# A hybrid decoder layer on one core: weight sums of the first four feed forward gemms made during the in-projection, and embedding stores on ScalarE's queue

## The chip, the cores and the metric

The kernel runs on one core of a Trainium2 chip. The metric is the device time of one execution in microseconds (us). A core has five engines with a queue of their own each: TensorE (PE in the profile, with its weight loads as PEld), VectorE (DVE), ScalarE (ACT), GpSimd (POOL) and SyncE (SP, which here only issues DMAs). Every queue is worked off in order; engines wait for one another through semaphores.

## The reference, cut to what matters

One layer, D_MODEL = 1024, 1024 rows, float32, D_FF = 2816:

```python
h = rms_norm(x, norm1_g)
proj = h @ w_in                                  # columns for three causal mixers
mixed = concat(gated_deltanet(...), multiscale_pool(...), short_gated_conv(...))
x = x + mixed @ w_out
h = rms_norm(x, norm2_g)
ff = silu(h @ w_gate) * (h @ w_up)
x = x + ff @ w_down
x = x + sigmoid(x @ ple_gate) * (p @ ple_proj)   # p: per-layer input embedding, 256 wide
return rms_norm(x, final_g)
```

## The kernel before, in words

All matrices stand transposed, 128 features on the partitions and the 1024 rows in two halves of 512. A float32 product is made of three matmuls, hi·hi, hi·lo and lo·hi: each operand is split into `hi`, a copy that ScalarE rounds (`act.copy` into an fp32r tile), and `lo`, the rest, which VectorE subtracts (`vec.tensor_tensor`). A matmul takes 128 x 128 weights and 512 columns.

The stages follow each other: the in-projection, with DeltaNet, pooling and short convolution woven into it; the out-projection (16 gemms of 24 matmuls, blocks of `w_out` split one ahead into `wh` and `wl`); the second norm; the feed forward gemms; the down-projection; the embedding gate and the last norm.

The feed forward is done by a 2 x 2 block scheme with seven products in place of eight. Its right operands `B[0]` to `B[6]` (four pieces each) come from the normed input: `B[0]`, `B[1]` from the first half of the rows alone, `B[2]` to `B[6]` from both. `norm2(1)` (L1231) makes them on VectorE in this order, and its events `t2_ev` and `t4_ev` stand for the end of what `B[2]` and `B[6]` are made of. The left operands of one of 22 gemms (`jobs`, even: two blocks of `w_gate`, odd: two of `w_up`) are two raw quarters a11, a12, four sums of quarters, and a22, with the numbers i = 0 to 6. The sums are four GpSimd instructions over 128 x 512, in `sums(n)` (L1338). Each of the seven operands is then split by ScalarE and VectorE into one of 8 `op` tiles, in the order of the list `uses`, and one operand feeds 12 matmuls, so a gemm has 84 matmuls.

`EARLY = 4`: the first four gemms start with products 0 and 1 (`head1`, `head2`), which need only `B[0]`, `B[1]`, while `norm2(1)` runs. Then come `embed(0)` (the first half of p @ ple_proj, 48 matmuls, whose operands go through the same `op` tiles), then products 2 to 6 of gemms 0 and 1 alternately (`p6`, `p7`, `p5`, `tail1`, `tail2`; the last needs `B[6]`), then `embed(1)`, then gemms 2 to 21. The sums of gemms 2 and 3 wait for `t4_ev`, and the first four `op` tiles used are given back only after `t4_ev` (`held_ops`, L1408). `embed_evac` (L1445) copies a block of 128 x 512 out of PSUM on ScalarE and stores it to `pp_d` in DRAM by SyncE; it is read again at the embedding gate.

Raw weight blocks of 512 KB lie in `wr` tiles: two in the pool `stg` (`ra_slots`) and four in `ffp` (`rb_slots`). Gemms 0 and 1 hold two `rb` slots each until their last operand is split; every later gemm holds one of each. `down_sums(p)` (L1579) takes two `rb` slots too, loads two blocks of `w_down`, makes four sums on GpSimd and stores them to `wd_d`; `a_sums(p)` (L1562) makes four GpSimd sums of the feed forward's activations, which SyncE stores to `a_d`. `after(n)` (L1664) starts one or the other behind gemm n.

The program order on every queue is written out by a planner, `Flow`: Python generators yield the time at which they go on by the planner's cost model, and a gemm's `fl.tick` advances its clock. The planner fixes the order of instructions; at run time each queue only waits for its semaphores. A DMA that SyncE can't issue yet, since its tile is not free, holds up all that stand behind it. Units of 128 x 512 in SBUF come from one pool of 69 (`gen`).

Of the kernel before, what the change touches and what calls it, by code (L numbers as in the profile page):

```python
# [9 lines left out]
F32 = mybir.dt.float32  # L10
F32R = mybir.dt.float32r
AF = mybir.ActivationFunctionType
ALU = mybir.AluOpType
# [8 lines left out]
NH = 4  # L22
NT = 8
NFF = 22
EPS = 1e-6

V_N1, V_N2, V_FG, V_TAP, V_STAP, V_PS, V_ON = 0, 8, 16, 24, 72, 78, 80
# [168 lines left out]
def kernel(  # L196
# [28 lines left out]
    x1_d = scr.tile([2, KT, P, HALF], F32, name="x1_d")  # L225
    a_d = scr.tile([7, NFF // 2, P, HALF], F32, name="a_d")
    wd_d = scr.tile([4, NFF // 2, P, HALF], F32, name="wd_d")
    pp_d = scr.tile([2, KT, P, HALF], F32, name="pp_d")

    uid = [0]  # L230
# [5 lines left out]
    def unit(dtype=F32, shape=(P, HALF)):  # L236
        return gen.tile(list(shape), dtype, tag="u", name=nm("u"))

    def load(src):
        t = unit(shape=tuple(src.shape))  # L240
        sync.dma_start(out=t, in_=src)
        return t
# [11 lines left out]
    def free(ps):  # L254

        if id(ps) in held:
            held.remove(id(ps))
            fl.spawn(mm_slots.later(), fl.left() - 0.15)

    def store(dst, src, ev):  # L260

        sync.dma_start(out=dst, in_=src)
        ev.set(2.6)
        yield 0
# [46 lines left out]
    class Weights:  # L311
# [5 lines left out]
        def fetch(self):  # L317
            if self.srcs and len(self.raw) < 2:
                src, kind = self.srcs.pop(0)
                raw = stg.tile([P, KT, P], F32, tag="wr", name=nm("wr"))  # L320
                sync.dma_start(out=raw, in_=src)  # L321
                self.raw.append((raw, kind))
# [183 lines left out]
    def gates(ab_sb):  # L506
# [75 lines left out]
        for pr in range(2):  # L582
            batch = list(zip(todo, ws))[4 * pr:4 * pr + 4]
            for (h, hf), w in batch:
                for t in range(4):
                    vec.tensor_scalar(out=w[:, t, :], in0=w[:, t, :], scalar1=gc[:, hf * 4 + t, h:h + 1],
                                      scalar2=None, op0=ALU.subtract)
                act.activation(out=w, in_=w, func=AF.Abs)
                yield from fl.calm(pr, "act", "vec")
            for (h, hf), w in batch:  # L590
                act.activation(out=w, in_=w, func=AF.Exp, scale=-1.0)
                fl.spawn(store(q4(w_d[h, hf]), w, w_done[h]), fl.left())
            yield fl.left()


    def conv_evac(tap, dst, ready):
# [690 lines left out]
    NPR = NFF // 2  # L1287
    jobs = []
    for p in range(NPR):
        jobs += [(w_gate[2 * p], w_gate[2 * p + 1]), (w_up[2 * p], w_up[2 * p + 1])]  # L1290


    EARLY = 4
    uses = []
    for n in range(0, EARLY, 2):
        uses += [(n, 0), (n + 1, 0), (n, 1), (n + 1, 1)]

    uses += [(-1, q) for q in range(4)]
    uses += [(b, i) for i in range(2, 7) for b in range(2)]
    uses += [(-1, q) for q in range(4)]  # L1300
    for n in range(2, len(jobs)):
        more = EARLY <= n + 1 < len(jobs)
        uses += [(n, 2), (n, 3), (n, 4)] + [(n + 1, 0)] * more + [(n, 5)] + [(n + 1, 1)] * more + [(n, 6)]
# [11 lines left out]
    def raw_tile(hp):  # L1315
        return hp.tile([P, KT, P], F32, tag="wr", name=nm("wr"), bufs=2 if hp is stg else 4)

    def weights():
        raws = [[None, None, Event(fl), Event(fl)] for _ in jobs]

        def fetch(n, c):
            raws[n][c] = raw_tile(ffp if c or n < 2 else stg)
            sync.dma_start(out=raws[n][c], in_=jobs[n][c])
            raws[n][2 + c].set(5.0)

        def loader():
            todo = [(n, c) for n in range(2) for c in range(2)] + [(2, 0), (3, 0), (2, 1), (3, 1)]
            todo += [(n, c) for n in range(4, len(jobs)) for c in range(2)]
            for n, c in todo:
                if n >= 2 and c == 0:  # L1330
                    yield out_w
                    yield from ra_slots.take()
                else:
                    yield from rb_slots.take()
                fetch(n, c)
                yield 0.1

        def sums(n):  # L1338
            if 2 <= n < EARLY:
                yield t4_ev  # L1340
            yield raws[n][2]
            yield raws[n][3]
            ra, rb = raws[n][0:2]
            a11, a12, a21, a22 = ra[:, 0:4], ra[:, 4:8], rb[:, 0:4], rb[:, 4:8]
            s1 = unit(shape=(P, 4, P))
            pool.tensor_tensor(out=s1, in0=a21, in1=a22, op=ALU.add)
            pool.tensor_tensor(out=a21, in0=a11, in1=a21, op=ALU.subtract)
            own[n] = (a11, a12, a11, a21, s1, a12, a22)
            yield split_ev[n]
            pool.tensor_tensor(out=a11, in0=s1, in1=a11, op=ALU.subtract)  # L1350
            pool.tensor_tensor(out=a12, in0=a12, in1=a11, op=ALU.subtract)
            yield fl.left()
            sum_ev[n].set()

        own = [None] * len(jobs)
        split_ev, sum_ev = events(len(jobs)), events(len(jobs))
        fl.spawn(loader())
        started = 0
        todo = [q for n, q in uses if n < 0]

        def proj(q):
            t = unit(shape=(P, 4, P))
            sync.dma_start(out=t.rearrange("p (k j) c -> p k (j c)", k=2),
                           in_=ple_proj[:, :, 2 * P * q:2 * P * q + 2 * P].rearrange("k p c -> p k c"))
            return t, fl.now + 4.0

        ahead = [proj(todo.pop(0)) for _ in range(2)]
        for n, i in uses:
            while started < len(jobs) and started <= n + 1:
                fl.spawn(sums(started))  # L1370
                started += 1
            yield from op_slots.take()
            if n < 0:
                raw, at = ahead.pop(0)
                yield max(0.0, at - fl.now)
                if todo:
                    ahead.append(proj(todo.pop(0)))
            elif i < 2:
                yield raws[n][2]
                raw = raws[n][0][:, 4 * i:4 * i + 4]  # L1380
            else:
                if i == 2:
                    yield t2_ev
                yield sum_ev[n]
                raw = own[n][i]
            hi, lo = op_tile()
            act.copy(out=hi, in_=raw)
            vec.tensor_tensor(out=lo, in0=raw, in1=hi.bitcast(F32), op=ALU.subtract)
            ops.append((hi, lo))
            if n >= 0 and i == 1:  # L1390
                split_ev[n].set()
            if op_free:
                op_free.pop().set()
            raw = None
            if i == 6:
                own[n] = raws[n] = None
                (rb_slots if n < 2 else ra_slots).give()
                rb_slots.give()
            yield 0.3

    def next_op():
# [43 lines left out]
    def embed_evac(ps, hf, j):  # L1445
        t = unit()
        act.copy(out=t, in_=ps)
        free(ps)
        yield fl.left()
        yield from store(pp_d[hf, j], t, pp_ev[hf][j])  # L1450

    def embed(hf):
        fl.until(pH_ev[hf])
        for q in range(4):
            hi, lo = next_op()
            for b in range(2):
                ps = bank()
                products(ps, [(hi[:, 2 * k + b], lo[:, 2 * k + b]) + tuple(pH[hf][k]) for k in range(2)])
                fl.spawn(embed_evac(ps, hf, 2 * q + b), 0.3)
            op_used()  # L1460
        pH[hf] = None
# [117 lines left out]
    def down_sums(p):  # L1579

        yield from rb_slots.take()
        yield from rb_slots.take()
        da, db = (raw_tile(ffp).rearrange("p k c -> p (k c)") for _ in range(2))
        sync.dma_start(out=da, in_=w_down[2 * p])
        sync.dma_start(out=db, in_=w_down[2 * p + 1])
        s1 = unit()
        yield 4.0
        a11, a21, a12, a22 = da[:, 0:HALF], da[:, HALF:], db[:, 0:HALF], db[:, HALF:]
        pool.tensor_tensor(out=s1, in0=a21, in1=a22, op=ALU.add)
        pool.tensor_tensor(out=a21, in0=a11, in1=a21, op=ALU.subtract)  # L1590
        pool.tensor_tensor(out=a11, in0=s1, in1=a11, op=ALU.subtract)
        pool.tensor_tensor(out=a12, in0=a12, in1=a11, op=ALU.subtract)
        yield fl.lag("pool")
        for i, t in enumerate((a11, a21, s1, a12)):
            sync.dma_start(out=wd_d[i, p], in_=t)
        rb_slots.give()
        rb_slots.give()
# [66 lines left out]
    def after(n):  # L1664
        p, _, ab = todo[n]
        if ab:
            fl.spawn(a_sums(p, *ab), 0.4)
        else:
            fl.spawn(down_sums(p), 2.0)

    g = [t[1] for t in todo]
    for n in range(0, EARLY, 2):
# [2 lines left out]
            f(g[n + 1])  # L1675
    embed(0)
    fl.spawn(p_proc(1))
    for f in (Gemm.p6, Gemm.p7, Gemm.p5, Gemm.tail1, Gemm.tail2):
        f(g[0])
        f(g[1])  # L1680
    after(0)
    after(1)
    embed(1)
    for n in range(2, len(g)):
        nxt = g[n + 1] if EARLY <= n + 1 < len(g) else None
        if n + 1 == len(g):
# [220 lines left out]
```

## Time and profile before

| what | value |
|---|---|
| median of 3 runs | 1254.97 us (1253.57 to 1256.13) |
| profiled execution, its own time | 1256.83 us |
| its span | 1255.2 us |
| TensorE busy | 1217.2 us, 97% of the span |
| VectorE, ScalarE, GpSimd busy | 64%, 42%, 25% |

The profile is of one execution. Stretches are given in microseconds from the start of its span. In a row, `x90` is a count of instructions; `<-DVE u` names the engine and the tile that ended a wait; the clock is TensorE's granted clock as a share of its full speed; SPq is SyncE's queue, where a row gives the time of issue. Names of tiles have no numbers, so `u` is any of the 69 units.

### The profile page before, as it was taken

How to read it: one execution, taken by the hardware profiler on the slowest of the kernel's cores; microseconds unless marked ns; L12 is line 12 of the kernel's file. 1: busy time of each engine (PE TensorE's matmuls, PEld its weight loads, DVE VectorE, ACT ScalarE, POOL GpSimd, SP SyncE). 2: the span in 40 equal slices, each digit the busy share in tenths (PEclk: the TensorE clock that was granted, in tenths of full speed). 3: DMA queues.
4: the chain of work that ended last, by engine and by line, in shares of the span. 5: the costliest groups of instructions: out<-in, count | busy, mean ns of one | idle time of the engine just before them, and what ended most of it. 6: DMA issues, size and time to landing. Idle time of an engine off the chain costs nothing.

```text
span 1255.2 us, 17243 instructions
## 1 busy us (share of the span) xinstructions
PE 1217.2 (97%) x6103; PEld 1006.8 (80%) x6103; DVE 801.1 (64%) x1381; ACT 527.5 (42%) x1114; POOL 308.2 (25%) x257
## 2 busy tenths in 40 slices
PE   8999999999999989978999999999999999999996
PEld 6778888888877878857888888888888888888886
DVE  8675886985766587865555555555547565553674
ACT  7256343254244343632333333333346444443553
POOL 7100001100010030074655655556530000000001
PEclk9999999999999999988999999999999999999998
DMA  6046353332335752345453543444369666563452
GB/s 223 17 144 187 102 136 101 107 101 85 100 130 166 253 182 84 126 158 180 154 188 127 191 145 151 160 176 143 132 221 373 205 213 198 174 197 116 146 181 94
DMA packets 112806, 196.63 MB, mean 157 GB/s; under 512 B 23696, under 2 KB 38864, under 8 KB 112720
## 3 DMA queue, kind: packets, MB, share of 16 engines
q1 hardware_dynamic: 112720, 195.53, 47.0%
q8 instruction: 48, 0.79, 0.3%
q14 instruction: 38, 0.31, 0.1%
HBM read 141.19 MB, written 54.30 MB: 156 GB/s over the span
## 4 chain that ended last, share of the span: by engine, by line
PE 52%; DVE 1%; DMA 1%; issue 0%; ACT 0%; POOL 0%; SPq 0%; POOLq 0%; ACTq 0%
PE dn L347 36%; PE mm L347 16%; DMA wr<-in_ple_gate_dram 1%; DVE u L140 1%; ACT u L140 0%; POOL u L140 0%; POOLq L1902 0%; DVE dl L140 0%; SPq L1817 0%; SPq L1798 0%; DVE ms L140 0%; POOL rs L140 0%; POOLq L140 0%; SPq L321 0%; ACTq L140 0%
## 5 line engine op out<-in xcount | busy, mean ns | idle before, releaser
L347 PE MATMUL dn<-u,op 128*128 128x512 f32 x1632 | 382.3, 394 | 12.8 <-DVE u L140 10.5
L347 PEld LDWEIGHTS dn<-u,op 128*128 128x128 f32 x1632 | 310.5, 191 | 80.5 <-DVE u L140 12.1
L347 PE MATMUL mm<-u,wh 128*128 128x512 f32 x1104 | 354.3, 402 | 5.4 <-DVE u L140 3.6
L140 DVE TENSOR_TENSOR u<-u,u 128x512 fp32r<-128x512 f32 (+2 forms) x358 | 234.6, 694 | 47.1 <-ACT u L140 40.4
L347 PEld LDWEIGHTS mm<-u,wh 128*128 128x128 f32 x1104 | 202.7, 190 | 49.1 <-DVE u L140 5.4
L347 PE MATMUL mm<-u,wl 128*128 128x512 f32 x552 | 217.9, 395 | 4.1 <-DVE wl L140 4.1
L140 ACT CAST u<-u 128x512 fp32r<-128x512 f32 x214 | 125.3, 620 | 137.4 <-DVE u L140 60.3
L140 DVE TENSOR_TENSOR op<-wr,op 128x512 fp32r<-128x512 f32 x132 | 121.0, 921 | 95.4 <-ACT op L140 93.8
L347 PE MATMUL dn<-u,u 128*128 128x512 f32 (+2 forms) x850 | 159.5, 336 | 0.0
L347 PEld LDWEIGHTS dn<-u,u 128*128 128x128 f32 (+1 forms) x850 | 123.6, 170 | 24.1 <-issue 0.5
L347 PEld LDWEIGHTS mm<-u,wl 128*128 128x128 f32 x552 | 104.7, 190 | 27.9 <-DVE wl L140 5.8
L140 ACT CAST op<-wr 128x512 fp32r<-128x512 f32 x132 | 81.5, 620 | 93.4 <-PE dn L347 58.8
L140 ACT ACTIVATE u<-u 128x512 f32<-128x512 f32 (+1 forms) x137 | 82.0, 605 | 88.3 <-DVE u L140 86.4
L347 PE MATMUL mm<-u,u 128*128 128x512 f32 (+1 forms) x522 | 112.0, 352 | 2.0 <-DVE u L140 1.5
L140 DVE TENSOR_TENSOR u<-dn,u 128x512 f32<-128x512 f32 x93 | 64.0, 689 | 73.6 <-PE dn L347 64.8
L140 DVE TENSOR_TENSOR wl<-wr,wh 128x512 fp32r<-128x512 f32 (+2 forms) x96 | 68.0, 711 | 65.0 <-ACT wh L140 64.4
L140 ACT COPY u<-dn 128x512 f32<-128x512 f32 (+4 forms) x99 | 47.7, 482 | 139.1 <-PE dn L347 139.1
L140 POOL TENSOR_TENSOR rs<-ms,mhalf 128x4 f32<-128x4 f32 (+1 forms) x7 | 6.6, 942 | 396.2 <-DVE ms L140 396.2
L347 PEld LDWEIGHTS mm<-u,u 128*128 128x128 f32 x522 | 85.5, 189 | 16.3 <-DVE u L140 2.1
L140 POOL TENSOR_TENSOR u<-u,u 128x512 f32<-128x512 f32 (+1 forms) x61 | 84.1, 1392 | 33.0 <-DVE u L140 20.4
L140 DVE TENSOR_TENSOR u<-mm,u 128x512 f32<-128x512 f32 x60 | 41.2, 687 | 48.2 <-PE mm L347 45.2
L140 ACT CAST wh<-wr 128x512 fp32r<-128x512 f32 (+2 forms) x96 | 57.7, 608 | 29.0 <-issue 12.5
(164 smaller groups left out, 1178.7 us busy)
## 6 DMA issues: line engine op xcount, KB each, us to landing
a_d<-u SPq DMA_DIRECT2D x77, 256.0 KB, 2.8
u<-a_d SPq DMA_DIRECT2D x77, 256.0 KB, 3.7
wr<-in_w_gate_dram SPq DMA_DIRECT2D x22, 512.0 KB, 4.6
wr<-in_w_up_dram SPq DMA_DIRECT2D x22, 512.0 KB, 4.5
wr<-in_w_down_dram SPq DMA_DIRECT2D x22, 512.0 KB, 4.9
u<-wd_d SPq DMA_DIRECT2D x44, 256.0 KB, 3.0
wr<-in_w_in_dram SPq DMA_DIRECT2D x21, 512.0 KB, 3.6
wd_d<-wr SPq DMA_DIRECT2D x33, 256.0 KB, 2.4
```

The lines of the kernel that those rows point to most:

```text
L140: return f(*a, **kw)
L347: pe.matmul(out=out, lhsT=lhsT, rhs=rhs, start=start, stop=stop, **kw)
```

## The change: what it does

A generator `early_sums`, started when the first norm's second half is done, loads the blocks of gemms 0 to 3 in quarters, makes their four sums each on GpSimd and stores them to `sd_d` in DRAM. At the feed forward, the operands of these gemms come from DRAM: tiles with key "a" (a11, a12), "s" (two sums), "d" (a22) and "e" (two pieces of `ple_proj`, which had units before) are fetched into the four `rb` slots in the order of use, each given back after its second split. From gemm 4 on, an even gemm holds both `ra` slots and an odd one two `rb` slots. `embed(1)` stands ahead of the two `tail2` of gemms 0 and 1. Embedding stores are issued by ScalarE. `down_sums` of pairs 0 and 1 go behind gemms 4 and 8.

```diff
+    def early_sums():
+        yield rs_done[1]
+        for n in range(EARLY):
+            wa, wb = gate_up(n)
+            a11, a12, a21, a22 = (load(w[:, r]) for w in (wa, wb) for r in (slice(0, 4), slice(4, 8)))
+            s1 = unit(shape=(P, 4, P))
+            yield 4.0
+            pool.tensor_tensor(out=s1, in0=a21, in1=a22, op=ALU.add)
+            pool.tensor_tensor(out=a21, in0=a11, in1=a21, op=ALU.subtract)
+            pool.tensor_tensor(out=a11, in0=s1, in1=a11, op=ALU.subtract)
+            pool.tensor_tensor(out=a12, in0=a12, in1=a11, op=ALU.subtract)
+            yield fl.left() + 2.0
+            for i, t in enumerate((a11, a21, s1, a12)):
+                sync.dma_start(out=sd_d[n, i // 2, :, 4 * (i % 2):4 * (i % 2) + 4], in_=t)
+            sd_ev[n].set(3.0)
+
+    fl.spawn(early_sums())
...
     uses += [(-1, q) for q in range(4)]
-    uses += [(b, i) for i in range(2, 7) for b in range(2)]
-    uses += [(-1, q) for q in range(4)]
+    uses += [(b, i) for i in range(2, 6) for b in range(2)]
+    uses += [(-2, q) for q in range(4)]
+    uses += [(b, 6) for b in range(2)]
...
+        def fetch_early(key):
+            t = tiles[key][0] = raw_tile(ffp)
...
+            elif key[0] == "s":
+                sync.dma_start(out=t, in_=sd_d[key[1], key[2]])
+            elif key[0] == "d":
+                sync.dma_start(out=t[:, 0:4], in_=jobs[key[1]][1][:, 4:8])
+            else:
+                sync.dma_start(out=t, in_=jobs[key[1]][0])
+            tiles[key][1].set(4.5)
+
         def fetch(n, c):
-            raws[n][c] = raw_tile(ffp if c or n < 2 else stg)
+            raws[n][c] = raw_tile(ffp if n % 2 else stg)
...
+        def loader(odd):
+            for key in tiles if odd else ():
+                if key[0] == "s":
+                    yield sd_ev[key[1]]
+                yield from rb_slots.take()
+                fetch_early(key)
                 yield 0.1
+            yield out_w
+            for n in range(EARLY + odd, len(jobs), 2):
+                for c in range(2):
+                    yield from (rb_slots if odd else ra_slots).take()
+                    fetch(n, c)
+                    yield 0.1
 
         def sums(n):
-            if 2 <= n < EARLY:
-                yield t4_ev
...
     def embed_evac(ps, hf, j):
         t = unit()
         act.copy(out=t, in_=ps)
+        act.dma_start(out=pp_d[hf, j], in_=t)
         free(ps)
-        yield fl.left()
-        yield from store(pp_d[hf, j], t, pp_ev[hf][j])
+        pp_ev[hf][j].set(4.0)
+        yield 0
...
         if ab:
             fl.spawn(a_sums(p, *ab), 0.4)
-        else:
+        elif n >= EARLY:
             fl.spawn(down_sums(p), 2.0)
+            if n < 3 * EARLY and n % 4 == 0:
+                fl.spawn(down_sums(n // 4 - 1), 20.0)
...
-    for f in (Gemm.p6, Gemm.p7, Gemm.p5, Gemm.tail1, Gemm.tail2):
+    for f in (Gemm.p6, Gemm.p7, Gemm.p5, Gemm.tail1):
         f(g[0])
         f(g[1])
+    embed(1)
+    g[0].tail2()
+    g[1].tail2()
     after(0)
     after(1)
-    embed(1)
```

## Rows read from the trace of the kernel before

**Rows 1.** Chain that ended last, pieces of a later gemm: start, us.

```profile
597.13 16.32 PE dn L347 x72
613.45 2.72 PE mm L347 x12
```

**Rows 2.** Stretches: PE busy, PEld, DVE, ACT, POOL (counts), clock, DMA share, GB/s.

```profile
440.00:460.00 20.00, 16.10 (x64) 12.61 (x63) 17.74 (x20) 8.81 (x18) 9.70 (x7) 0.91 0.45 152
...
500.00:520.00 20.00, 20.00 (x90) 16.57 (x89) 17.23 (x29) 16.87 (x32) 0.00 (x0) 1.00 0.36 132
520.00:540.00 20.00, 16.14 (x65) 12.43 (x64) 19.44 (x27) 6.29 (x12) 7.68 (x5) 0.92 0.42 132
540.00:560.00 20.00, 20.00 (x82) 16.16 (x80) 13.18 (x10) 7.93 (x15) 16.53 (x12) 0.91 0.36 109
560.00:580.00 20.00, 11.73 (x35) 8.88 (x35) 6.98 (x9) 4.64 (x8) 8.27 (x6) 0.74 0.73 273
```

**Rows 3.** What PE waited for, 430 to 475: total, times, longest.

```profile
PE mm L347 <- DVE wl L140: 3.9, 2, 2.7
```

**Rows 4.** What PE waited for, 530 to 600.

```profile
PE dn L347 <- DVE u L140: 10.5, 3, 6.2
PE dn L347 <- ACT u L140: 1.6, 1, 1.6
```

**Rows 5.** Timeline of all engines, 441 to 452: start, us.

```profile
441.94 1.78 DVE L140 TENSOR_TENSOR u<-u,u 128x512 fp32r<-128x512 f32 x1
...
443.13 1.75 POOL L140 TENSOR_TENSOR wr<-u,wr 128x512 f32<-128x512 f32 x1
...
451.02 0.68 DVE L140 TENSOR_TENSOR wl<-wr,wh 128x512 fp32r<-128x512 f32 x1
...
451.75 0.80 PE L347 MATMUL mm<-u,wl 128*128 128x512 f32 x1 [2.66 <-DVE wl L140]
```

**Rows 6.** DVE by form, 485 to 530, no sums on POOL: total, mean ns.

```profile
L140 DVE TENSOR_TENSOR u<-u,u 128x512 fp32r<-128x512 f32 x18 | 12.2, 687 | 0.0
```

**Rows 7.** DVE by form, 530 to 560, beside sums on POOL.

```profile
L140 DVE TENSOR_TENSOR op<-wr,op 128x512 fp32r<-128x512 f32 x6 | 8.1, 1395 | 2.6 <-ACT op L140 2.6
```

**Rows 8.** Timeline of all engines, 530 to 575.

```profile
532.17 1.52 POOL L140 TENSOR_TENSOR u<-wr 128x512 f32<-128x512 f32 x1 [49.22 <-ACT op L140]
...
537.64 6.17 PE L347 MATMUL dn<-u,op 128*128 128x512 f32 x14 [2.20 <-DVE u L140]
...
543.65 11.08 PE L347 MATMUL mm<-ph,op 128*128 128x512 f32 x48
...
563.18 0.58 ACT L140 COPY u<-mm 128x512 f32<-128x512 f32 x1 [7.27 <-DMA pp_d<-u]
...
566.41 5.04 PE L347 MATMUL dn<-u,op 128*128 128x512 f32 x12 [6.23 <-DVE u L140]
...
573.48 20.93 PE L347 MATMUL dn<-u,op 128*128 128x512 f32 x84 [2.04 <-DVE u L140]
```

**Rows 9.** SP's issues in the same stretch: start, us.

```profile
545.85 0.33 SPq L262 DMA_DIRECT2D pp_d<-u  x1
...
555.96 2.03 SPq L1323 DMA_DIRECT2D wr<-in_w_gate_dram  x2
...
564.06 0.56 SPq L262 DMA_DIRECT2D pp_d<-u  x1
```

**Rows 10.** POOL by form, 580 to 920.

```profile
L140 POOL TENSOR_TENSOR wr<-wr,wr 128x512 f32<-128x512 f32 x25 | 35.4, 1415 | 2.0
```

**Rows 11.** One stretch of the in-projection, columns as in group 2.

```profile
44.00:94.00 50.00, 48.79 (x221) 35.91 (x220) 36.60 (x88) 26.62 (x64) 2.94 (x8) 1.00 0.32 101
```

**Rows 12.** What PE waited for, 40 to 100.

```profile
PE mm L347 <- DVE u L140: 1.2, 1, 1.2
```

**Rows 13.** DMA issues: count, KB each, median us from issue to landing.

```profile
wr<-in_w_gate_dram SPq DMA_DIRECT2D x22, 512.0 KB, 4.6
```

**Rows 14.** Stretch where the down-projection starts, columns as in group 2.

```profile
940.00:960.00 20.00, 20.00 (x90) 16.57 (x89) 13.37 (x19) 7.54 (x13) 1.68 (x2) 1.00 0.96 339
```

More of the change, by code (lines that the diff above doesn't have):

```diff
@@ L24 @@
 NFF = 22
+EARLY = 4
 EPS = 1e-6
@@ L227 @@
     wd_d = scr.tile([4, NFF // 2, P, HALF], F32, name="wd_d")
+    sd_d = scr.tile([EARLY, 2, P, KT, P], F32, name="sd_d")
     pp_d = scr.tile([2, KT, P, HALF], F32, name="pp_d")
@@ L593, in gates, with gate_up @@
             yield fl.left()
+    def gate_up(n):
+        w = w_up if n % 2 else w_gate
+        return w[n - n % 2], w[n - n % 2 + 1]
+    sd_ev = [Event(fl) for _ in range(EARLY)]
+    def early_sums():
[14 more added lines that the diff above has]
+    fl.spawn(early_sums())
     def conv_evac(tap, dst, ready):
@@ L1289 @@
     for p in range(NPR):
-        jobs += [(w_gate[2 * p], w_gate[2 * p + 1]), (w_up[2 * p], w_up[2 * p + 1])]
-    EARLY = 4
+        jobs += [gate_up(2 * p), gate_up(2 * p + 1)]
     uses = []
@@ L1319, in weights @@
         raws = [[None, None, Event(fl), Event(fl)] for _ in jobs]
+        src = {}
+        for n, i in uses:
+            if n < 0:
+                src[n, i] = (("e", n, i // 2), i % 2)
+            elif n < EARLY:
+                src[n, i] = (("s", n, i // 2 - 1) if i in (2, 3, 4, 5) else ("d", n) if i == 6 else ("a", n), i % 2)
+        tiles = {}
+        for key, _ in map(src.get, (u for u in uses if u in src)):
+            if key not in tiles:
+                tiles[key] = [None, Event(fl), 1 if key[0] == "d" else 2]
@@ new lines, in fetch_early @@
+        def fetch_early(key):
+            t = tiles[key][0] = raw_tile(ffp)
+            if key[0] == "e":
+                for h in range(2):
+                    c = 2 * P * (2 * key[2] + h)
+                    sync.dma_start(out=t[:, 4 * h:4 * h + 4].rearrange("p (k j) c -> p k (j c)", k=2),
+                                   in_=ple_proj[:, :, c:c + 2 * P].rearrange("k p c -> p k c"))
+            elif key[0] == "s":
[5 more added lines that the diff above has]
+            tiles[key][1].set(4.5)
@@ L1321, in fetch @@
         def fetch(n, c):
-            raws[n][c] = raw_tile(ffp if c or n < 2 else stg)
+            raws[n][c] = raw_tile(ffp if n % 2 else stg)
             sync.dma_start(out=raws[n][c], in_=jobs[n][c])
             raws[n][2 + c].set(5.0)
[L1326 to L1332, printed above, removed]
-                else:
-                    yield from rb_slots.take()
-                fetch(n, c)
-                yield 0.1
+        def loader(odd):
[4 more added lines that the diff above has]
+                fetch_early(key)
+                yield 0.1
+            yield out_w
[4 more added lines that the diff above has]
+                    yield 0.1
@@ L1356, in weights @@
         split_ev, sum_ev = events(len(jobs)), events(len(jobs))
[L1357 to L1367, printed above, removed]
+        fl.spawn(loader(1))
+        fl.spawn(loader(0))
+        started = EARLY
         for n, i in uses:
@@ L1372, in weights @@
             yield from op_slots.take()
[L1373 to L1377, printed above, removed]
+            key = None
+            if (n, i) in src:
+                key, h = src[n, i]
+                if i == 2:
+                    yield t2_ev
+                yield tiles[key][1]
+                raw = tiles[key][0][:, 4 * (0 if key[0] == "d" else h):][:, 0:4]
             elif i < 2:
@@ L1381, in weights @@
             else:
-                if i == 2:
-                    yield t2_ev
                 yield sum_ev[n]
@@ L1389, in weights @@
             ops.append((hi, lo))
-            if n >= 0 and i == 1:
-                split_ev[n].set()
+            raw = None
             if op_free:
                 op_free.pop().set()
-            raw = None
-            if i == 6:
+            if key:
+                tiles[key][2] -= 1
+                if not tiles[key][2]:
+                    tiles[key][0] = None
+                    rb_slots.give()
+            elif i == 1:
+                split_ev[n].set()
+            elif i == 6:
                 own[n] = raws[n] = None
-                (rb_slots if n < 2 else ra_slots).give()
-                rb_slots.give()
+                for _ in range(2):
+                    (rb_slots if n % 2 else ra_slots).give()
             yield 0.3
@@ L1667, in after @@
             fl.spawn(a_sums(p, *ab), 0.4)
-        else:
+        elif n >= EARLY:
             fl.spawn(down_sums(p), 2.0)
+            if n < 3 * EARLY and n % 4 == 0:
+                fl.spawn(down_sums(n // 4 - 1), 20.0)
     g = [t[1] for t in todo]
```

## The prediction

> **What bounds the kernel now.** I read the stretches first, then TensorE's waits, then the timeline around the longest of them. TensorE is the bound: a later feed forward gemm has 84 matmuls in 16.32 + 2.72 = 19.04 us [rows 1], 0.2267 us each, and from 573 on it runs through 84 of them in 20.93 us without a gap [rows 8]. An undisturbed stretch of 20 us holds 90 matmuls [rows 2]. So the number that counts is not the busy time but how many matmuls a stretch lacks of 90. The stretch from 440 lacks 26; those from 520, 540 and 560 lack 25, 8 and 55, together 88 [rows 2]. At 0.2267 us that is 5.9 and 19.9 us, 25.9 us in all. The waits of TensorE in the two places are only 3.9 and 12.1 us [rows 3, 4]; the other 9.9 us are slow matmuls around the waits, with the granted clock at 0.91, 0.92, 0.91 and 0.74 where the undisturbed stretch has 1.00 [rows 2], and 0.80 us for the first matmul after a wait [rows 5]. What removes a wait gives back this part too.
>
> Why TensorE waits there. At 440 it needs `wl`, the low part of a `w_out` block. VectorE makes it, but VectorE is behind: GpSimd makes the sums of gemms 0 and 1 at the same time, and a subtraction beside a GpSimd sum takes 1.78 us [rows 5], or 1.395 us in the mean of a group, against 0.687 us when GpSimd is idle [rows 6, 7]. At 532 GpSimd starts the sums of gemms 2 and 3 just when VectorE must finish `B[6]`, and TensorE stands until 537.6 [rows 8]. At 560 the cause is another one: ScalarE waits 7.27 us for a unit whose embedding store is late, since SyncE issues in order and the store stands behind weight fetches that wait for their tiles [rows 8, 9]. Behind that copy on ScalarE stands the next operand's split, and TensorE waits 6.23 us and then 2.04 us [rows 8].
>
> **The change part by part.**
>
> *Sums of gemms 0 and 1 leave the out-projection.* Eight GpSimd instructions go; VectorE then runs at 0.687 us. The second late `wl` was 2.66 us late [rows 5]; three subtractions stretched by 1.09 us (1.78 - 0.69) ahead of it account for that, and VectorE worked beside GpSimd from before 442 on. So both waits go: -5.9 us, with 3.9 (the waits alone) as the weakest case. The tile loads stay: four of 512 KB at the same place.
>
> *Sums of gemms 2 and 3 leave the place of `B[6]`, and `embed(1)` goes ahead of `tail2`.* The 48 matmuls of `embed(1)`, 11.08 us [rows 8], now run while VectorE finishes `B[6]`; TensorE was served `B[6]` at 537.6 after waits of at most 1.6 and 2.2 us at this place [rows 4, 8], so 11 us is more than enough even with VectorE as it was. The operands need one load from DRAM in place of the sums: four slots with two operands each are 8 operands ahead at 2.72 us of TensorE each, against 4.6 us for a load [rows 13]. *Embedding stores on ScalarE's queue, `down_sums` later.* A store can't stand behind a fetch any more. Together these take the causes of all three waits: -19.9 us; weakest case, one of the causes stays (below).
>
> *What the stores cost on ScalarE.* An issue takes 0.33 to 0.56 us on SyncE [rows 9]; no row shows one on ScalarE. `embed(0)` brings eight, 2.6 to 4.5 us, into the stretch from 500, where ScalarE is busy for 16.87 of 20 us and VectorE for 17.23 [rows 2] and the splits of `B[2]` to `B[5]` go through both just ahead of TensorE. 3.1 us of ScalarE are free; between 0 and 4.5 us I take 2, since the issues come in a bunch. `embed(1)`'s eight fall where ScalarE is busy for 6.29 of 20 us [rows 2]: nothing, and 4.5 at most if that cover were gone.
>
> The Trainium skill, "DMA: Bandwidth & Descriptors", section "Issuing engines are not separate DMA queues", says that issuing from several engines only saves the sequencer's time to initiate a DMA. By that rule the move of 16 stores would be worth some 16 x 0.33 = 5 us of SyncE, which is no bound, thus nothing, and the 560 wait would stay; the row of 7.27 us shows a store waiting ahead of its issue, which the rule doesn't speak of.
>
> *Sums go into the in-projection.* 16 sums of 1.415 us [rows 10] are 22.6 us of GpSimd, in four bursts: the generator starts at about 44, and one round is 4 + 5.7 + 2 = 11.7 us by its own waits and the four sums, which ends at 91. GpSimd is busy there for 2.94 of 50 us [rows 11], so its own time is hidden. Also 16 loads and 16 stores of 256 KB; the 16 engines are busy for a share of 0.32 there [rows 11], and SyncE's 32 issues of 0.33 to 0.56 us are 11 to 18 us of a queue that is mostly waiting: hidden, unless a store waits for a late sum. A `w_in` block is fetched two blocks ahead, and a block is 10.9 us of TensorE, so a few us of that cost nothing. But VectorE is slowed here now. Each sum stretches a subtraction by 1.395 - 0.687 = 0.71 [rows 6, 7] up to 1.78 - 0.69 = 1.09 us [rows 5, 6]: 11.3 to 17.4 us. VectorE is busy for 36.6 of 50 us [rows 11], so 13.4 us are free, and TensorE already waited once for VectorE there, 1.2 us [rows 12]. What doesn't fit is 17.4 - 13.4 = 4.0 us: I take 4, with 0 and 17.4 as bounds. A gain is excluded, since nothing is removed here.
>
> The Trainium skill, "SBUF — State Buffer", section "Who interferes with whom", says that a VectorE instruction with two SBUF inputs and a GpSimd instruction that reads SBUF exclude each other for a whole instruction. The trace agrees (0.687 against up to 1.78 us). It speaks against this change: by it each of 16 sums could block for its full 1.415 us, 22.6 us, and the sum below would come out 5.2 us worse beyond the 17.4.
>
> *A new order behind it.* The planner lays out all later instructions anew. TensorE's other waits in the in-projection are about 1.2 us each [rows 12]; two more such waits, 2.4 us, could come or one or two go. I take 2, bounds -2 and 4.
>
> *Later `down_sums`, other slots.* Two more `down_sums` must pass among gemms 4 to 21, and an odd gemm holds two of the four slots that they need, so the last ones may run into the start of the down-projection, where the DMA engines are at 0.96 and 339 GB/s [rows 14]. Each brings 1 MB in and 1 MB out, 6 us at that rate; operands are loaded up to seven steps of 2.72 us ahead, so most is hidden: I take 1, bounds 0 and 6.
>
> Sum: -5.9 - 19.9 + 2 + 4 + 2 + 1 = -16.8 us. The profiled execution took 1256.83 us, so 1240.0; it stands 1.9 us above the median of the runs, which makes 1238.2: **1238 us**.
>
> **The rivals.**
>
> (a) *VectorE pays in the in-projection* what it is spared later: the bursts don't spread over its free time, and 12 to 17.4 us in place of 4 reach TensorE: 1246 to 1251. For it: VectorE is at 73% there and a wait exists already [rows 11, 12]. Against: TensorE is still busy for 48.79 of 50 us there [rows 11], and the bursts have pauses of about 6 us for the next loads and stores.
>
> (b) *The 560 wait stays*, because units run out whoever issues the stores: the 55 missing matmuls there are 12.5 us, and 1238 + 12.5 gives 1250.5. For it: ScalarE's copy waited for a unit to be stored [rows 8]. Against: the issue was what was late [rows 9]. The Trainium skill's rule on issuing engines, cited above, comes out here too.
>
> (c) *The late `down_sums` starve the start of the down-projection*: 5 us beyond the 1 taken, 1243.
>
> (d) *Slower than before: the steady gemms lose their cover.* An even gemm now has both blocks in the two `ra` slots, so both are fetched only when the gemm two before has split its last operand. From there to the split of the first sum are 8 operands, 21.8 us. Needed are a load of 4.6 us, about 2 more for the second block, and four sums, 5.7 us: 12.3, and 11.3 more if GpSimd has an `a_sums` and a `down_sums` ahead: 23.6 us. TensorE then lives on the operands split ahead. It decides from 16.8 / 9 = 1.9 us a pair of gemms; at 3 us a pair, 27 us, the time is 1265. Against: up to eight `op` tiles of 2.72 us lie between.
>
> (e) *The change doesn't do what it says*: TensorE finds another operand late at both places and gains nothing: 1255.
>
> **How the numbers follow.** The chances: forecast 0.58 (its own range 1231 to 1244), (a) 0.12, (b) 0.12, (c) 0.08, (d) 0.06, (e) 0.04. A difference of 0.2%, 2.5 us, is about what a measurement of this kernel can tell from none. The forecast, (c), (b) and most of (a) (0.10) are faster: 0.88. Half of (e) and the rest of (a) are the same: 0.04. (d) and half of (e) are slower: 0.08. The range reaches down to all 25.9 us without a cost (1229) and up to (b) and (a): 1230 to 1251; outside lie (d), (e) and little else.
>
> **What would show it.** Right: the stretches from 440 and from 520 to 580 hold 90 matmuls at clock 1.00; 16 GpSimd sums stand between 47 and 95, and VectorE's subtractions there take 1.1 to 1.8 us; the 48 matmuls of `embed(1)` come ahead of 24 of `tail2` without a wait between; the stores to `pp_d` are on ScalarE's queue. Wrong: TensorE waits over 5 us in the in-projection; a wait of ScalarE for `pp_d` remains; gemms 4 to 21 take more than 19.04 us.

## The result: 1.6% slower

The changed kernel takes 1276.6 us (median of 4 runs, 1272.3 to 1277.8) against 1255.6 for the kernel before beside it: ratio 1.0163, 95% interval 1.0135 to 1.0190. The forecast was 1238, range 1230 to 1251.

Both traces hold 6103 matmuls, so the start of the n-th one can be compared. This table, worked out from the two traces, says how much later the changed kernel has become in each part (the times are those of the kernel before), beside the prediction's terms. Each part is read from one execution; where a kernel was left as it was, a part still moved by about 1 us (the out-projection: -0.9 in e12, +1.3 in e15).

| part | matmuls | predicted, us | measured, us |
|---|---|---|---|
| in-projection, to 145 | to 624 | +4, +2 | +18.0 |
| attention, to 418 | to 2400 | 0 | +1.4 |
| out-projection, to 459 | to 2560 | -5.9 | -5.9 |
| norm and first gemms, to 504 | to 2760 | 0 | +4.6 |
| `embed(1)` and T4, to 584 | to 3024 | -19.9, +2 | -11.5 |
| to 715 | to 3600 | 0 | 0.0 |
| gemms to 828 | to 4100 | +1 | +12.4 |
| rest | to 6102 | 0 | +0.5 |
| sum | | -16.8 | +19.5 |

By this table forecast and result are 36.3 us apart: 12.0 in the in-projection, 11.4 among the gemms to 828, 6.4 at T4, 4.6 ahead of it at 459 to 504, and 1.9 in the rest.

**Where it was won and lost.** Stretches of the changed kernel, columns as in [rows 2]:

```profile
60.00:80.00 20.00, 17.16 (x71) 13.62 (x70) 17.71 (x41) 7.81 (x18) 5.35 (x5) 0.91 0.09 25
80.00:100.00 20.00, 16.57 (x69) 13.07 (x69) 10.62 (x20) 5.00 (x17) 6.17 (x6) 0.91 0.88 293
100.00:120.00 20.00, 15.42 (x61) 11.41 (x60) 12.08 (x24) 10.88 (x25) 7.53 (x5) 0.91 0.64 215
...
440.00:460.00 20.00, 20.00 (x91) 16.31 (x91) 12.57 (x24) 8.82 (x16) 1.01 (x1) 1.00 0.75 269
480.00:500.00 20.00, 17.81 (x73) 14.00 (x73) 12.65 (x21) 6.88 (x13) 4.24 (x3) 0.91 0.59 180
520.00:540.00 20.00, 20.00 (x90) 16.57 (x89) 13.97 (x23) 14.76 (x27) 0.00 (x0) 1.00 0.58 204
540.00:560.00 20.00, 17.83 (x77) 13.84 (x75) 17.01 (x29) 10.54 (x19) 0.00 (x0) 1.00 0.51 161
560.00:580.00 20.00, 16.93 (x72) 13.36 (x72) 10.75 (x13) 7.87 (x14) 10.67 (x8) 1.00 0.61 200
580.00:600.00 20.00, 19.85 (x80) 16.26 (x81) 9.30 (x14) 6.11 (x10) 2.20 (x2) 0.91 0.28 101
...
780.00:800.00 20.00, 15.08 (x55) 11.86 (x56) 11.68 (x12) 7.16 (x13) 14.01 (x10) 0.83 0.27 92
```

The stretch from 440 is full, at clock 1.00, as forecast [rows 2, 3]. At T4, which comes up to 20 us later here, the four stretches from 520 lack 0, 13, 18 and 10 matmuls of 90, together 41, in place of 88.

**What TensorE waited for.** Its waits in the changed kernel, 60 to 120, 475 to 600 and 700 to 940 (total, times, longest):

```profile
PE mm L349 <- ACT wh L141: 3.3, 1, 3.3
PE dn L349 <- DVE gg L141: 2.8, 1, 2.8
PE mm L349 <- DVE pre L141: 2.6, 1, 2.6
...
PE dn L349 <- DVE u L141: 4.1, 2, 2.1
PE mm L349 <- ACT u L141: 1.4, 2, 1.0
PE dn L349 <- ACT u L141: 1.3, 1, 1.3
...
PE dn L349 <- ACT op L141: 8.9, 2, 7.0
```

The first three are in the in-projection, where the kernel before had one wait of 1.2 us [rows 12]; all waits from 40 us to the end of this part add up to 13.0 us here. All three signs that the prediction named for "wrong" are there: this one, 3.1 us of ScalarE's waiting for `pp_d` between 500 and 600, and gemms that take longer than 19.04 us. The timeline in the in-projection (start, us) shows how one of them comes about:

```profile
43.95 2.90 DVE L141 TENSOR_SCALAR u<-ident,rs 128x128 f32<-128x128 f32 x4 [0.34 <-POOL rs L141]
...
82.52 2.55 SPq L617 DMA_DIRECT2D sd_d<-u  x4
85.11 2.80 SPq L243 DMA_DIRECT2D u<-in_w_gate_dram  x4
...
93.12 5.39 POOL L141 TENSOR_TENSOR u<-u,u 128x512 f32<-128x512 f32 x4 [17.92 <-DMA u<-in_w_gate_dram]
98.45 0.10 POOL L141 MEMSET pre<- 128x3 f32 x1
98.59 0.72 ACT L141 ACTIVATE u<-pre,vt 128x512 f32<-128x512 f32 x1 [9.55 <-POOL pre L141]
99.34 0.75 DVE L141 SCALAR_TENSOR_TENSOR u<-pre,vt,u 128x512 f32<-128x512 f32 x1 [7.71 <-ACT u L141]
```

GpSimd stands 17.92 us for the third gemm's loads, which SyncE issues late; a memset of 128x3 stands behind the four sums; ScalarE needs it, VectorE needs ScalarE, TensorE the `wh` that ScalarE makes next. From the rows alone this looked like a matter of waits. The experiments say that waits alone are not it.

### The profile page after: what moved, and what is told of

Its sections match the earlier page's. It is cut to its first block, busy times and chain, and to the rows that moved or that the text cites. A ratio compares the mean times of both kernels' runs of the same rounds, so it can differ in the third digit from the quotient of the medians.

```text
span 1274.7 us, 17275 instructions
## 1 busy us (share of the span) xinstructions
PE 1221.9 (96%) x6103; PEld 1006.7 (79%) x6103; DVE 800.8 (63%) x1381; ACT 527.4 (41%) x1112; POOL 318.4 (25%) x257
## 4 chain that ended last, share of the span: by engine, by line
PE 47%; DMA 2%; issue 1%; POOL 1%; DVE 1%; ACT 0%; SPq 0%; POOLq 0%; ACTq 0%
PE dn L349 32%; PE mm L349 15%; POOL wr L141 1%; DMA wd_d<-wr 1%; DVE u L141 1%; DMA wr<-in_ple_gate_dram 1%; POOL u L141 1%; DMA wr<-in_w_up_dram 1%; DVE op L141 0%; DMA wr<-in_w_gate_dram 0%; ACT u L141 0%; ACT op L141 0%; SPq L1646 0%; POOLq L1957 0%; DVE dl L141 0%
## 5 line engine op out<-in xcount | busy, mean ns | idle before, releaser
L141 DVE TENSOR_TENSOR op<-wr,op 128x512 fp32r<-128x512 f32 x144 | 135.3, 948 | 104.4 <-ACT op L141 100.1
L141 POOL TENSOR_TENSOR u<-u,u 128x512 f32<-128x512 f32 (+1 forms) x77 | 110.6, 1448 | 134.7 <-ACT u L141 78.5
L141 ACT CAST op<-wr 128x512 fp32r<-128x512 f32 x144 | 87.1, 619 | 89.4 <-PE dn L349 46.8
```

Source lines behind the costliest of these rows:

```text
L141: return f(*a, **kw)
```

## The experiments

Delays by part below are worked out as in the table. In e1, e11 and e13 the first four gemms compute something else, as each expectation says.

**e1: no sums.** The 16 GpSimd sums are left out, the loads and stores kept.

> The changed kernel with the 16 GpSimd sums of the early generator left out: its 16 loads and 16 stores stay, and raw quarters are stored where sums belong, so the feed forward's first four gemms compute something else. Theory (GpSimd's queue is what costs the in-projection 17 us: a sum that waits for a late load holds up the small memset behind it, and through ScalarE the splits): the loss up to TensorE's 480th matmul against the kernel before falls from 17.8 us to 4 us or less, and the time from 1276 to about 1262. Rival (SyncE's queue and the 8 MB of traffic are the cost): the loss stays at 14 us or more, the time at 1273 or more.

1255.9 us, ratio 1.0009 (0.9997 to 1.0021). The in-projection's loss is gone (-0.7 by 145): it hangs on the sums, not on the 32 DMAs of the early sums. The +12.4 at 715 to 828 stays, so it has another cause.

**e2: sums 2 us behind the gates.**

```diff
-        yield rs_done[1]
+        yield gates_done
+        yield 2.0
```

> The changed kernel with the early generator started only behind the gates' own row loads on SyncE's queue, so that no load of a quarter stands behind SyncE's wait for the gates; same 16 sums, now between about 85 and 140. Theory (a late load at the head of GpSimd's queue): no wait of ScalarE for the memset of pre above 3 us, the loss in the in-projection is 5 us or less, the time about 1264. Rival (the sums slow VectorE wherever they stand, by 11 to 17 us as the prediction bounded it): the loss stays at 11 us or more, the time at 1270 or more.

1278.8, ratio 1.0189 (1.0171 to 1.0208): missed. The loss moves with the sums, +20.2 by 145, and it comes in two longer waits of TensorE, 8.5 us for `wl` and 6.3 us for `wh`. The gates' instructions of 128x32 are over here before the first sum. VectorE stands 10.3 us for a load of `w_d`, and SyncE's stores of sums stand 14.1 us in all for GpSimd.

**e3 and e4: raw tiles of the later gemms as before** (block a in a `ra` slot, b in an `rb` slot, one order of fetches), on the changed kernel and on e2.

> The changed kernel with the raw tiles of gemms 4 to 21 as before the change: first block in the two tiles of stg, second in the four of ffp, so that an odd gemm and a run of down_sums no longer need two of the same four slots each. The two later runs of down_sums stay. Theory (odd gemms' fetches are held up by down_sums that hold slots): the 12.4 us lost between 760 and 835 go, TensorE's wait of 7.0 us for a split behind GpSimd is gone, time about 1264. Rival (two more runs of down_sums are too much for GpSimd there): a wait of 5 us or more stays in the gemms 4 to 21, time 1272 or more.

> The changes of the second and third experiment together. If the two losses are independent, the gains add: about 1252, and with the in-projection's loss at 5 us and the gain of the early gemms at 14 us it is 1 to 5 us faster than the kernel before. If one only hides the other, 1260 or more.

1294.4 (ratio 1.0314, 1.0289 to 1.0339) and 1292.2 (1.0301, 1.0277 to 1.0325): both missed. Going back to the old slots, with the later `down_sums` kept, does not help. In e3 the loss at 715 to 828 grows to +27.2, with one wait of TensorE of 23.3 us; in this stretch of e3 GpSimd is full and TensorE empty:

```profile
800.00:820.00 20.00, 2.22 (x4) 1.33 (x5) 2.27 (x2) 2.70 (x5) 19.21 (x16) 0.50 0.85 294
```

**e5 to e8: longer waits, slots of their own, and the sums of gemm 4.** e5 waits 10 and 8 us in place of 4 and 2 and starts 12 us behind the gates. e6 divides the four `rb` slots once the early tiles are in:

```diff
+        def share():
+            for sl in (od_slots, od_slots, dn_slots, dn_slots):
+                yield from rb_slots.take()
+                sl.give()
...
-                    yield from (rb_slots if odd else ra_slots).take()
+                    yield from (od_slots if odd else ra_slots).take()
...
-        yield from rb_slots.take()
-        yield from rb_slots.take()
+        yield from dn_slots.take()
+        yield from dn_slots.take()
```

e7 is both, and e8 adds to `sums(n)` a wait for `t4_ev` where n is 4.

> The whole computation is kept; the early sums start behind the gates plus 12 us, wait 10 us instead of 4 after their loads are issued and 8 us instead of 2 before their stores are issued. Theory (an in-order engine stands still because a sum waits for a late load, or a store or load issue on SyncE stands behind a store that waits for a late sum): with the longer waits nothing stands, the loss by the end of the in-projection and the attention falls from 19.5 us to at most 5, and the time is about 1262. Rival (each sum slows VectorE by 0.7 to 1.1 us wherever it is put, and TensorE pays 16 of these): the loss there stays at 11 us or more, the time is 1268 or more.

> The whole computation is kept; of the four rb slots the down_sums get two of their own and the odd gemms the other two, from the moment the early tiles have been loaded. Theory (the 12.4 us lost at 760 to 833 is a backlog of down_sums, which start at 688 instead of 532 because the odd gemms' prefetch holds the slots, and then run back to back on GpSimd ahead of the gemm sums): down_sums come evenly again, the 12.4 us fall to at most 3, the time is about 1265. Rival (the new fetch order of the steady gemms alone costs it): the loss at 760 to 833 stays at 8 us or more, 1273 or more. The in-projection's loss of some 19 us is not touched by this one.

> The two edits of e5 and e6 together, whole computation kept. If both causes are right and independent: 1276.6 - 14 - 11 = about 1251, thus no slower than before; if only one holds, about 1263; if neither, 1277.

> e7 and in addition the sums of gemm 4 wait until B[4] is made, as the sums of gemms 2 and 3 did before the change; whole computation kept. Theory (the 3.9 us lost at about 490 are VectorE slowed by GpSimd's sums of gemm 4 while it makes the down-projection's input): that loss goes to 1 us or less, 1247 to 1248. Rival (the stores issued on ScalarE's queue cost it): the loss stays and the time is that of e7.

Medians 1271.0, 1265.7, 1261.6 and 1254.2; ratios 1.0123 (1.0092 to 1.0155), 1.0085 (1.0056 to 1.0114), 1.0055 (1.0025 to 1.0086) and 0.9992 (0.9971 to 1.0013). e6 came out as its theory said (about 1265); e7 (1251 if both causes were right) and e8 (1247 to 1248) missed. e6 settles the 12.4: in e6, e7 and e8 it is 0.0. The first ops of the eleven `down_sums` stand at 550, 583, 622 and so on in the kernel before, some 38 us apart; in the changed kernel the first is at 699.8 and seven stand between there and 813.8, 19 us apart; in e6 the first is at 629.9. The changed kernel at the loss, where GpSimd runs through `down_sums` and late gemm sums, and below it the same stretch of e6:

```profile
784.22 1.14 ACT L141 CAST op<-wr 128x512 fp32r<-128x512 f32 x2 [4.87 <-POOL wr L141]
...
784.89 15.31 PE L349 MATMUL dn<-u,op 128*128 128x512 f32 x55 [6.99 <-ACT op L141]
```

```profile
780.00:800.00 20.00, 20.00 (x90) 16.58 (x89) 12.19 (x16) 7.07 (x12) 12.54 (x9) 1.00 0.38 120
```

e8 bears on the +4.6 at 459 to 504: it falls to 1.2, and to 1.3 in e9 and e10, which have the same edit; in the variants that keep both the new fetch order and gemm 4's sums where they were, it is 1.9 to 6.6. In the changed kernel GpSimd starts gemm 4's sums there, and VectorE's subtractions for `op` take 1.4 us each beside them. They stand ahead of an input of the second norm (not of the down-projection, as the expectation has it), for which TensorE waits 2.09 us:

```profile
488.49 1.60 POOL L141 TENSOR_TENSOR u<-wr 128x512 f32<-128x512 f32 x1 [38.71 <-DVE op L141]
...
489.50 2.83 DVE L141 TENSOR_TENSOR op<-wr,op 128x512 fp32r<-128x512 f32 x2 [0.57 <-ACT op L141]
...
494.47 1.02 PE L349 MATMUL dn<-ones,u 128*128 128x1 f32 x8 [2.09 <-DVE u L141]
```

Single times of e7 and e8 scatter more (1252 to 1269, 1250 to 1261), so this is read from the part, not from the time, and e8's trace is of its slowest execution. e5 speaks for its rival: the loss is 8.3 by 145 but 15.2 by 418, so longer waits shift the loss more than they take it away.

**e9 and e10: the sums at 275 to 370.** e9 is e8 with one number changed, 200 us in place of 12; e10 is e9 with the embedding's stores on SyncE.

> e8 with one number changed: the early sums start 200 us behind the gates instead of 12, so at about 285, where GpSimd is busy for 1 to 2.3 of 20 us in the kernel before and VectorE for 7.9 to 15.4; whole computation kept. Theory (the sums cost only where TensorE, ScalarE and VectorE hand each other work tile by tile and SyncE's queue is full, as in the in-projection and the first attention pair): the 9 to 17 us that e5, e7 and e8 still lose by 210 go, and nothing comes in their place: about 1245, between 1238 and 1249. Rival (16 sums cost TensorE about half a microsecond each wherever they stand): 1251 or more.

> e9 with the embedding stores issued on SyncE again, as before the change; whole computation kept. Theory of the prediction (the late issue behind weight fetches made the wait of 7.27 us): a wait of ScalarE for a stored unit comes back near 560, 5 to 12 us slower than e9. Rival (the gain came from the place of the embedding's second half, and the issue on ScalarE only costs its time): within 2.5 us of e9, or faster by the 2.5 us that the changed kernel loses at 543 to 552.

e9: 1241.7 us, **ratio 0.9885 (0.9872 to 0.9899): faster than both kernels, and all of the computation is there**. The same 16 sums, 1.57 us each here, cost 1.8 us up to 418 (-0.6 by 145, +1.2 by 418). Of 14.8 us won, 5.9 are at the out-projection and 11.7 at T4. Two of e9's stretches, and the longest wait that is left there, from TensorE's timeline:

```profile
520.00:540.00 20.00, 16.58 (x70) 12.46 (x68) 16.25 (x26) 10.17 (x19) 3.73 (x2) 1.00 0.51 171
540.00:560.00 20.00, 16.98 (x73) 13.43 (x73) 11.68 (x14) 8.12 (x14) 10.67 (x8) 1.00 0.72 237
```

```profile
559.93 6.46 PE L349 MATMUL dn<-u,op 128*128 128x512 f32 x27 [2.43 <-DVE u L141]
```

e10: 1244.7, ratio 0.9901 (0.9885 to 0.9918). That is 3.0 us above e9, between what the theory and the rival had said. The intervals overlap, and ScalarE's waits for `pp_d` are 3.7 us against 3.0. The wait of 7.27 us [rows 8] doesn't come back.

**e11 and e13: what in the sums costs.** e11 makes 16 sums of full length that wait for nothing, on a scratch unit; e13 leaves all the waits and makes the sums short:

```diff
-            pool.tensor_tensor(out=s1, in0=a21, in1=a22, op=ALU.add)
+            pool.tensor_tensor(out=a22[:, 0:1, 0:4], in0=a21[:, 0:1, 0:4], in1=a22[:, 0:1, 0:4], op=ALU.add)
```

> The changed kernel, but its 16 early sums work on one scratch unit of zeros, made once, and so wait for no load, and no store waits for them; the raw quarters are stored in their place, so the first four gemms compute something else. GpSimd still makes 16 sums of the same shape in the same part. Theory (what costs 17 us in the in-projection are the waits in the order of the queues: sums for late loads, stores for sums, and all that stands behind them): the loss by 150 us falls to at most 5, the time is 1258 to 1263. Rival (each sum holds VectorE up by 0.7 to 1.1 us beside it): the loss stays at 11 us or more, the time is 1270 or more.

> The changed kernel, but each of the 16 early sums works on 4 of 512 columns, so GpSimd still waits for the same loads, and the stores and all behind them for GpSimd, but VectorE has next to nothing beside it; the rest of each quarter is stored as it was loaded, so the first four gemms compute something else. If the 17 us are about half waits in the order of the queues and half the sums' own hold on VectorE (as the 9 us left in e11 suggest): 6 to 10 us lost by 150 us, the time 1263 to 1268. If the waits alone make it: 15 us or more, 1272 or more. If the sums' own work alone makes it: at most 3 us, 1257 to 1260.

e11: 1265.0, ratio 1.0070 (1.0054 to 1.0085), +8.7 by 145, between the two theories. e13: 1258.6, ratio 1.0022 (1.0009 to 1.0034), -0.2 by 145, with GpSimd waiting up to 14.3 us for a load; that is its third case, the sums' own work. (Its trace is of an execution 2.8 us faster than its median, so the part may stand somewhat too low.) So the waits cost nothing where the sums are short. e11 isn't the counterpart that it was meant to be: its sums read one tile, take 1.14 us in place of 1.36, and stand elsewhere. How much longer VectorE's instructions take, from 40 us to the end of the in-projection, against the same forms in the kernel before, can be worked out from the traces: 8.0 us in the changed kernel, 4.4 in e11, 5.8 in e2, nothing in e1 and e13. So e11 has about half of the loss with about half of the stretching. The stretch 40 to 125 of the kernel before, the changed one, e11 and e13, in this order:

```profile
40.00:125.00 85.00, 83.79 (x406) 65.71 (x405) 55.34 (x158) 45.07 (x105) 7.64 (x15) 1.00 0.41 128
```

```profile
40.00:125.00 85.00, 72.44 (x314) 52.84 (x313) 51.33 (x110) 34.27 (x84) 27.11 (x26) 0.94 0.54 177
```

```profile
40.00:125.00 85.00, 77.80 (x355) 59.05 (x355) 55.48 (x140) 37.56 (x95) 24.90 (x28) 0.96 0.59 194
```

```profile
40.00:125.00 85.00, 83.51 (x402) 65.44 (x402) 55.58 (x158) 45.28 (x105) 11.89 (x31) 1.00 0.66 214
```

The counts in brackets are to be read: TensorE gets through 406, 314, 355 and 402 matmuls. VectorE is busy for 51 to 56 us in all four, yet gets through 158, 110, 140 and 158 instructions, in part because they take longer, in part because the stage is late. Its groups by form (total, mean ns), changed kernel, then e13:

```profile
L141 DVE TENSOR_SCALAR u<-ident,rs 128x128 f32<-128x128 f32 x8 | 3.8, 532 | 0.3 <-POOL rs L141 0.3
...
L141 DVE TENSOR_SCALAR pol<-s 128x32 f32<-128x32 f32 x1 | 1.2, 1153 | 0.0
L141 DVE TENSOR_TENSOR un<-un,den 128x32 f32<-128x32 f32 x1 | 1.0, 962 | 0.0
```

```profile
L141 DVE TENSOR_SCALAR u<-ident,rs 128x128 f32<-128x128 f32 x8 | 1.7, 280 | 0.3 <-POOL rs L141 0.3
L141 DVE TENSOR_TENSOR un<-un,den 128x32 f32<-128x32 f32 x1 | 0.2, 191 | 0.0
L141 DVE TENSOR_SCALAR pol<-s 128x32 f32<-128x32 f32 x1 | 0.2, 182 | 0.0
```

`pol<-s`, which takes 0.18 us alone, takes 1.15 us beside a sum.

**e14: the place alone.** The changed kernel, with 200 us behind the gates and nothing else.

> The changed kernel with one line changed: the early sums start 200 us behind the gates; slots, down_sums and the sums of gemm 4 as changed; whole computation kept. Theory (the losses add up): the 19.5 us before 400 go, the 3.9 at 490 and the 12.4 at 760 to 833 stay: 1276.6 - 19.5 = 1257, between 1254 and 1261. Rival (the later losses are a consequence of the early ones): 1245 or less.

1258.4, ratio 1.0014 (1.0001 to 1.0028), as the theory had it: +2.4 by 418, then +5.4 and +15.1 at the two later places (its trace is of its slowest execution, 1262.6). So the early loss can be taken out by itself, and the later ones stay.

**e12 and e15: the embedding alone, on the kernel before.** `embed(1)` ahead of the tails and its operand order; e12 with the stores on ScalarE's queue, e15 on SyncE's.

> The kernel before with one part of the change alone: the embedding's second half ahead of the tails that use T4, its stores on ScalarE's queue, and the operand order that goes with it; the sums of the first four gemms, the slots and the down_sums stay as before; whole computation kept. Theory (this part alone takes most of the 14 us that the changed kernel gains at 548 to 585): 1243, between 1240 and 1247. Rival (the gain needs the sums of gemms 2 and 3 out of this stretch): 1252 or more.

> e12 with the embedding's stores issued on SyncE as before the change; whole computation kept, old fetch order. Theory of the prediction (the store stands behind fetches in SyncE's order, and this made the wait at 560): 1252 to 1257, the gain of e12 is gone. Rival (the place of the embedding's second half makes the gain, whoever issues the stores): 1244 to 1249, as e12.

1246.9, ratio 0.9924 (0.9912 to 0.9937), and 1245.5, ratio 0.9923 (0.9905 to 0.9941): the order alone makes the gain at T4, 10.7 and 11.0 us from 504 to 584, whoever issues the stores and with the sums of gemms 2 and 3 still there. e12 lies at the upper end of what its theory had said, e15 where the rival had it.

## Why the prediction was wrong, by its steps

*Sums leave the out-projection: -5.9.* Right, in size too, the clock's part included: -5.8 or -5.9 in the changed kernel and in all its 13 variants.

*T4's place: -19.9.* A gain, but of 11.5, with the 2 of ScalarE's issues in it (11.7 in e9), and it was put down to three edits. The order of `embed(1)` alone makes 10.7 and 11.0 (e12, e15). What the sums of gemms 2 and 3 add by leaving can't be told from that: in the changed kernel and its variants this part is 9.2 to 13.3, on both sides of the order's own gain, and no run takes these sums out alone. Not all of the 88 missing matmuls came back: e9 lacks 37 of 180 in the stretches from 520 and 540, with waits for operands that are next in line (2.43 us for VectorE's `u`). A removed wait was priced as if nothing were late behind it.

*Stores on ScalarE's queue.* The step "a store can't stand behind a fetch any more" took the issuing queue for what had to change; e15 leaves the stores on SyncE and gains as much, with 2.3 us of ScalarE's waiting for `pp_d` in place of 7.3. In e15 SyncE issues the second half's eight stores between 533 and 543, and only two fetches stand among them, so that the new order takes the late issue away too. Whether the move alone would have done it in the old order, no run tests. On ScalarE an issue takes 0.33 us, and the engine stands 0.45 us around it, as at 529 in the changed kernel:

```profile
529.07 0.33 ACTq L1498 DMA_DIRECT2D pp_d<-u  x1
529.49 0.59 ACT L141 COPY u<-mm 128x512 f32<-128x512 f32 x1 [0.45 <-ACT u L141]
```

The Trainium skill, "DMA: Bandwidth & Descriptors", section "Issuing engines are not separate DMA queues", says that issuing from several engines saves only the sequencer's time. By that rule the move was worth nothing, and the runs agree (0.9924 in e12 against 0.9923 in e15; e9 and e10 overlap). The wait at 560 went all the same, with the order.

*The in-projection: +4, bounds 0 to 17.4.* The step that failed first. It set the stretch of VectorE's work (11.3 to 17.4 us) against VectorE's free time (13.4 us) and let only the rest through. Measured are 18.0, with the 2 of the new order in it. That this is about the upper bound and rival (a)'s price is luck: VectorE's work was stretched by 8.0 us, 0.5 a sum, less than the step's lowest. By the step's own subtraction that would cost nothing, and even all of it is less than half of what was lost. Free time in a 50 us mean doesn't hide a delay of an operand that is made just ahead of the matmul that needs it (TensorE waited for `gg`, `pre` and `wh`), and what is late is handed on through the queues. The term named that second case ("unless a store waits for a late sum") and priced it at nothing; here SyncE stands 7.0 us with a store for GpSimd, in e2 14.1. The term also priced 512-wide subtractions only, while instructions of 128x128 and 128x32 lose as much each; but e2, where the gates' 128x32 ones meet no sum, loses 20.2 all the same. Shown is that full-length sums at this place make the loss (e1, e13, e14). How it divides between VectorE and the queues was not taken apart and stays open.

*The place, not the number.* The same 16 sums cost 18.0 us in the in-projection and 1.8 in e9, though they stretch VectorE's work by about as much there (8.1 us, worked out as above, against 8.0). VectorE was nearly as busy there in the kernel before: 65 of 100 us from 280 to 380, 36.6 of 50 in [rows 11]. That TensorE's operands lie further ahead there is argued, not shown.

The Trainium skill, "SBUF — State Buffer", section "Who interferes with whom", says that a VectorE instruction with two SBUF inputs and a GpSimd instruction that reads SBUF shut each other out for a whole instruction. The `un<-un,den` of two SBUF tiles that grows from 0.19 to 0.96 us agrees. The TENSOR_SCALAR that grows from 0.18 to 1.15 reads one tile, though, for which the page sees contention only in VectorE's faster modes; whether it ran in one, no run here shows.

*Gemm 4's sums: nothing foreseen.* +4.6 (e8: 1.2). The loader now fetches gemm 4's blocks early, and its sums start at 488, between the two places from which those of gemms 0 to 3 had been taken.

*Later `down_sums`: +1.* The second step that failed, and nearly as costly. They were late, but cost 12.4, and not at the down-projection (rival (c)) but on GpSimd among the gemms. That is rival (d)'s place, by its smaller term (GpSimd has other sums ahead) and not by the even gemms' `ra` slots, which e6 leaves as changed: the first of eleven `down_sums` started 150 us late, because the odd gemms hold the slots, and the backlog then held up the sums of the gemms (e6: 0.0). The term priced the slots that an odd gemm holds as a delay of the last `down_sums`, not of the first.

## What to carry to other kernels

Work moved to an idle engine can be paid for by an engine that it slows and by all who wait in its queue: the mean busy share didn't tell the bad place from the good one here, so try several (19.4 us by 418 in the changed kernel against 2.4 in e14, which differs only in where the sums start). When a buffer pool is shared out anew, look at who comes later because of it, and what that will collide with when it catches up. Undo each part by itself: most of the gain that was put down to three edits came with one.

## What the runs showed of the hardware

Not every VectorE instruction that runs beside a GpSimd sum is held. Four sums of the changed kernel, and VectorE beside them:

```profile
106.36 6.34 POOL L141 TENSOR_TENSOR u<-u,u 128x512 f32<-128x512 f32 x4 [6.83 <-DMA u<-in_w_up_dram]
...
106.84 1.33 DVE L141 TENSOR_TENSOR wl<-wr,wh 128x512 fp32r<-128x512 f32 x1 [1.21 <-ACT wh L141]
...
109.78 0.68 DVE L141 TENSOR_TENSOR u<-mm,u 128x512 f32<-128x512 f32 x1
...
111.68 1.57 DVE L141 TENSOR_TENSOR wl<-wr,wh 128x512 fp32r<-128x512 f32 x1
```

`wl<-wr,wh`, with two tiles in SBUF, takes 0.69 us alone and 1.33 and 1.57 here; `u<-mm,u`, with one in SBUF and one in PSUM, takes its usual 0.68. An instruction that is held loses up to 1.0 us in the in-projection (a sum takes 1.36 in the mean), whatever its length: 128x32 from 0.18 to 1.15 us, 512-wide from 0.69 to 1.57. A queue that is mostly waiting isn't free: loads that SyncE issues at 85.1 us, behind a wait of 18.1 us for another engine, held GpSimd for 17.9 us and, through a 0.10 us memset, ScalarE for 9.6 us.
